# The instruction order of a two-block transformer kernel: a finer model in the ordering pass, and small matmuls issued in longer groups

## The chip, the core and the metric

The kernel runs on one core of one Trainium2 chip. The time is the device time of one execution in microseconds (us), the median of three runs. TensorE is PE in the profile (PEld are its weight loads), VectorE is DVE, ScalarE is ACT, GpSimd is POOL and SyncE, which issues the transfers here, is SP.

## The reference

Two transformer blocks work one after the other on x, 256 tokens of 1024 channels, in float32. The first block has two layers, the second one. Cut to what matters:

```python
for l in range(2):                       # first block
    z = rms_norm(x, norm1_g[l]) @ w_in[l]
    (cq, ckv, kpe, gq, gk, gv, glr, gr, su, gates) = split_in(z)
    o_a = mla_mixer(cq, ckv, kpe, ...)   # 8 heads of softmax attention
    o_b = gla_mixer(gq, gk, gv, glr, gr, ...)   # gated linear attention, 4 heads
    o_c = s5_mixer(su, ...)              # diagonal state space model + GLU
    g = sigmoid(gates + gate_b[l]).reshape(B, L, 3, D)
    x = x + (g0*(o_a @ w_br_mla) + g1*(o_b @ w_br_gla) + g2*(o_c @ w_br_s5)) @ w_out[l]
    x = x + square(relu(rms_norm(x, norm2_g[l]) @ w_ff1[l])) @ w_ff2[l]
# second block
q, k, v, glu_in, z_ga, z_gc = split(rms_norm(x, g_pre_mix) @ w_in_2)
y_attn = dilated_attention_mixer(q, k, v, rel_bias_table, w_attn_out)   # 24 heads in 3 groups
y_conv = conformer_conv_mixer(glu_in, ...)  # GLU, 31-tap causal conv, layer norm, silu, matmul
x = x + rms_norm((sigmoid(z_ga)*y_attn + sigmoid(z_gc)*y_conv) @ w_mix_out, g_post_mix)
x = x + rms_norm(swiglu_ffn(rms_norm(x, g_pre_ffn), ...), g_post_ffn)
```

## The kernel before

All big weights come as one stream of units, at most 128x1024 float32 each, in the order in which they are used. SP loads a unit into a tile `raw` (three buffers), ACT rounds it to the type fp32r as `wH` (L160, or L163 where a gain is multiplied in), and DVE makes the rest `wL = raw - wH` (L161, L164); `wH` and `wL` have four buffers each. Each product then takes three fp32r matmuls: high by high, high by low, low by high. L169 to L171 (`mm_f`) write 256 columns, L175 to L177 (`mm_t`) 512, and L1551 to L1553 are those of the convolution's output. Up to three units are fetched ahead (`AHEAD`).

Everything else on PE is plain float32 and small: transposes against the identity, attention scores and values, GLA's chunks, the S5 scan. This text calls those the small matmuls, and an unbroken row of them between two fp32r matmuls a run. They use PSUM tiles of one bank each from three pools: `mm` (2, the fp32r column units), `acc` (5) and `tr` (1).

What sets the order: `plan_layer` and `plan_second` walk the hand-written token lists `SCHED` and `SCHED2`. A token is a weight unit (`g1_6`, `co4`) or one step of a chain, and a chain is a generator that yields between steps: `l` GLA, `a` and `b` the two halves of the first block's attention, `s` S5, `h` the second block's attention, `c` the convolution, `n` its layer norm. The order in which instructions are written gives their priorities; the framework's ordering pass then plays the program through with a model of the engines and gives each engine, whenever it is free there, the ready instruction of best priority. So the order on an engine is not that of the text, and what a model believes to be ready decides it. On the chip each engine runs its list strictly in that order.

The small matmuls that the change touches, by function:

- `s5_tile_prep` (L466): eight transposes of `s5ep` (L478) in two groups of four, each into the one `tr` tile; ACT copies a group out to `ET` (L480) before the next can be written. Then eight small matmuls against `s5F` (L490).
- `gla` (L645), end: four transposes of `gla_og` per token half (L759).
- `mla_attn` (L861): per pair of heads four transposes of the q rows, copied out by ACT (L875), then four of the k rows (L872), through the one `tr` tile; scores (L884, L885); softmax; three transposes of `mla_p` per head (L906), copied out by L908; values (L912).
- `attn2` (L1401): per pair of heads and each of three groups, three transposes of the probabilities `sp` per head (L1448), copied out by L1450, then the values (L1457). L1436 is the exponential there, L1440 the scaling.

`mla_kv_evac` (L844) makes the normed k rows `mla_kn`: squares on ACT, the sum on DVE (L849), the inverse root on POOL (`rsq`, L184), two products on DVE (L856, L857). `s5_gelu` (L613) makes `s5gH` and `s5gL` for the S5 gate units (L621 to L627). `conv_gen` runs the 31 taps on DVE (L1321, L1318, L1314) with some products on ACT; `conv_ln` (L1352) norms the result: column sums (L1346), squares (L1363), the variance (L1349), the inverse root on POOL, its broadcast through PE (`tok_bcast`, L1333), a product on DVE (L1375), silu on ACT (L1378), and then the split `cH`, `cL` that the output units (L1551) read.

`k.behind(first, second)` adds a dependence: `second` becomes ready only after `first`.

Of the kernel before, what the change touches and what calls it, by code (L numbers as in the profile page):

```python
# [458 lines left out]
def s5_expand(k, dst, src):  # L459

    for g in range(2):
        rows, cols = slice(64 * g, 64 * g + 64), slice(16 * g, 16 * g + 16)
        k.nc.scalar.activation(dst[rows, :, :, cols], src[rows], AF.Copy)


def s5_tile_prep(k, st, ct):  # L466

    nc = k.nc
    js = slice(8 * ct, 8 * ct + 8)
    ep = k.s5ep  # L470
    s5_expand(k, ep[:, :, 0:1], st.b[:, js].unsqueeze(2))
    s5_expand(k, ep[:, :, 1:4], s5_powers(k, st, "s5e", 3, st.b, st.bs, ct, OP.add))
# [12 lines left out]
    s5_expand(k, k.s5F[:, :, 1:5], st.F[ct])  # L485
    Fq = k.s5F.rearrange("p (q c) s i -> p q c (s i)", c=2)
    ps = k.tr_tile()
    for c in range(2):
        for q in range(4):
            nc.tensor.matmul(ps[32 * q:32 * q + 32, 0:128], epq[:, q, c, 0:32], Fq[:, q, c, 0:128],  # L490
                             start=(c == 0), stop=(c == 1))
# [153 lines left out]
def gla(k, l, st):  # L645
# [97 lines left out]
    for tt in range(2):  # L743
# [8 lines left out]
        for h in range(4):  # L752
            hs = slice(h * P, (h + 1) * P)
            nc.vector.scalar_tensor_tensor(og[:, hs], po(tt, h), rs[:, h:h + 1], st.sr[:, tt, hs],
                                           op0=OP.mult, op1=OP.mult)
        yield
        pt = k.tr_tile()
        for h in range(4):
            nc.tensor.transpose(pt[:, h * P:(h + 1) * P], og[:, h * P:(h + 1) * P], k.ident)  # L759
# [83 lines left out]
def mla_kv_evac(k, l, st, t, ps, v):  # L843
# [13 lines left out]
    nc.vector.tensor_tensor(kn[:, :, 64:96], bcm(st.kr[:, t], 4), bcl(rh, 32), op=OP.mult)  # L857
# [4 lines left out]
def mla_attn(k, l, st, hf):  # L862

    nc = k.nc
    scale = 96.0 ** -0.5
    for pr in range(2):
        qk = []
        for src, g in ((st.qn[hf], "qhg"), (st.kn[hf], "khg")):
            ps = k.tr_tile()
            for hh in range(2):  # L870
                for t in range(2):
                    nc.tensor.transpose(ps[0:96, (2 * hh + t) * P:(2 * hh + t + 1) * P],  # L872
                                        src[t][:, 2 * pr + hh, :], k.ident)
# [5 lines left out]
        qT, kT = qk  # L879
        po = k.acc_tile()  # L880
        pb = []
        for hh in range(2):
            ps = k.acc_tile()
            nc.tensor.matmul(ps[:, 0:P], qT[0:96, hh, 0:P], kT[0:96, hh, 0:P], start=True, stop=True)  # L884
            nc.tensor.matmul(ps[:, P:3 * P], qT[0:96, hh, P:S], kT[0:96, hh, :], start=True, stop=True)  # L885
            sn = k.t2("mla_sn")
            mn = k.sm(2, "mmn")
            nc.vector.tensor_tensor_reduce(sn[:, 0:P], ps[:, 0:P], k.cmask[:, P:S], -scale, BIG, OP.add, OP.min,
                                           mn[:, 0:1])
            nc.vector.tensor_tensor_reduce(sn[:, P:3 * P], ps[:, P:3 * P], k.cmask, -scale, BIG, OP.add, OP.min,  # L890
                                           mn[:, 1:2])
            p = k.t2("mla_p")
            sm = k.sm(2, "msm")
            for b, cs in enumerate((slice(0, P), slice(P, 3 * P))):
                nc.scalar.activation(p[:, cs], sn[:, cs], AF.Exp, scale=-1.0, bias=mn[:, b:b + 1],
                                     accum_out=sm[:, b:b + 1])
            nc.vector.reciprocal(sm, sm)
            for b, cs in enumerate((slice(0, P), slice(P, 3 * P))):
                nc.vector.tensor_scalar(p[:, cs], p[:, cs], sm[:, b:b + 1], None, op0=OP.mult)
            pb.append(p)  # L900
            yield
        pTs = []
        for hh in range(2):
            pt = k.tr_tile()
# [4 lines left out]
        yield  # L909
        for j, (o, cs) in enumerate((((slice(0, S)), slice(0, S)), (slice(P, S), slice(S, 3 * P)))):  # L910
            for hh in range(2):
                k.behind(last, nc.tensor.matmul(po[64 * hh:64 * hh + 64, o], st.v[:, j, 4 * hf + 2 * pr + hh, :],  # L912
                                                pTs[hh][:, cs], start=(j == 0), stop=(j == 1)))
        yield
        k.split(st.moH[:, 2 * hf + pr], st.moL[:, 2 * hf + pr], po[:, 0:S])
        yield
# [485 lines left out]
def attn2(k, st, sp):  # L1402
# [28 lines left out]
    for i in hs:  # L1431
# [7 lines left out]
        for b, cs in enumerate(blocks):  # L1439
            nc.scalar.activation(s[i][:, :, cs], s[i][:, :, cs], AF.Copy, scale=sm[:, b:b + 1])  # L1440
        yield
    po = k.acc_tile()
    for g in range(3):
        pT = []
        for i in hs:
            pt = k.tr_tile()
            for b in range(3):
                nc.tensor.transpose(pt[:, b * P:(b + 1) * P], s[i][:, g, b * P:(b + 1) * P], k.ident)  # L1448
            pT.append(k.t2("pT2"))
            last = nc.scalar.activation(pT[i][:, 0:384].rearrange("p (b c) -> p b c", b=3)[:, :, ::-1],  # L1450
                                        pt[:, 0:384].rearrange("p (b c) -> p b c", b=3), AF.Copy)
        yield
        v = st.v2[g]
        for j, (o, cs) in enumerate(((slice(0, S), slice(0, S)), (slice(P, S), slice(S, 3 * P)))):
            for i in hs:
                h = 2 * sp + i
                k.behind(last, nc.tensor.matmul(po[rows[i], o], v[:, j, 64 * h:64 * h + 64], pT[i][:, cs],  # L1457
                                                start=(g == 0 and j == 0), stop=(g == 2 and j == 1)))
        yield
# [542 lines left out]
```

## Time and profile before

| | |
|---|---|
| median of 3 runs | 1453.17 us (1452.96 to 1453.40) |
| the profiled execution | 1451.78 us, of it span 1450.0 us |
| PE busy | 1402.2 us (97%), 10412 matmuls |
| DVE busy | 1012.9 us (70%) |
| ACT busy | 835.1 us (58%) |
| DMA | 243.1 MB, mean 168 GB/s |

A busy PE in this profile is an upper bound: matmuls overlap, so the length of one is more than the distance to the next. What a run of small matmuls costs is therefore read from the starts of the fp32r matmuls around it.

### The profile page before, as it was taken

The page shows a single profiled execution, that of the slowest core. Times are in us where ns is not written, and L with a number is a line of the kernel's source. Part 1 is how long each engine was busy: PE and PEld are TensorE (multiplying, and loading weights), DVE is VectorE, ACT ScalarE, POOL GpSimd, SP SyncE. Part 2 cuts the span into 40 slices and gives each one's busy share as a digit, 9 for nine tenths or more (in the row PEclk, how much of TensorE's full clock was granted, in tenths as well). Part 3 has the DMA queues.
Part 4 walks back from the last instruction along what each step waited for, and adds up shares of the span by engine and source line. Part 5 has one row for each costly group of instructions (what it writes and reads, how often), then busy time and mean ns, then how long its engine had stood idle before and what let it go on. Part 6 is the DMA issues. An engine that isn't in the chain of part 4 may idle for free.

```text
span 1450.0 us, 26147 instructions
## 1 busy us (share of the span) xinstructions
PE 1402.2 (97%) x10412; PEld 1272.1 (88%) x10412; DVE 1012.9 (70%) x1860; ACT 835.1 (58%) x1455; POOL 46.3 (3%) x51
## 2 busy tenths in 40 slices
PE   8999999999999999989999999999999999899998
PEld 6989889888899899888988999989888989689997
DVE  6987776689455667766566555579999846655555
ACT  6865566467754555455546444465678574544443
POOL 1000100000000000111000000000000000000000
PEclk9999999999999999999999999999999999999999
DMA  6622344555445552344456555565555445365553
GB/s 221 218 88 90 119 169 151 175 189 177 159 172 185 201 175 77 116 147 160 148 188 225 186 185 189 189 227 183 181 152 171 150 153 183 117 218 189 185 183 112
DMA packets 71058, 243.10 MB, mean 168 GB/s; under 512 B 7864, under 2 KB 11656, under 8 KB 70936
## 3 DMA queue, kind: packets, MB, share of 16 engines
q1 hardware_dynamic: 70936, 241.43, 48.8%
q8 instruction: 81, 1.33, 0.4%
q14 instruction: 41, 0.34, 0.1%
HBM read 237.17 MB, written 4.23 MB: 166 GB/s over the span
## 4 chain that ended last, share of the span: by engine, by line
PE 62%; DVE 13%; ACT 7%; issue 3%; DMA 2%; POOL 2%; POOLq 0%; DVEq 0%; ACTq 0%; SPq 0%
PE mm L169 11%; PE mm L171 11%; PE mm L170 11%; PE acc L175 7%; PE acc L177 7%; PE acc L176 7%; DVE wL L161 4%; ACT wH L160 2%; DVE cv L1321 2%; POOL rsq L184 2%; DMA raw<-in_wst_dram 2%; ACT sp L1436 1%; PE acc L553 1%; PE acc L1457 1%; ACT sp L1440 1%
## 5 line engine op out<-in xcount | busy, mean ns | idle before, releaser
L161 DVE TENSOR_TENSOR wL<-raw,wH 128x1024 fp32r<-128x1024 f32 (+1 forms) x410 | 496.1, 1211 | 260.4 <-ACT wH L160 259.0
L160 ACT ACTIVATE wH<-raw 128x1024 fp32r<-128x1024 f32 (+1 forms) x410 | 429.1, 1048 | 379.5 <-PE mm L170 184.7
L169 PE MATMUL mm<-hH,wH 128*128 128x256 f32 x1792 | 515.5, 288 | 5.0 <-ACT gt L1065 3.5
L171 PE MATMUL mm<-hH,wL 128*128 128x256 f32 x1792 | 510.4, 285 | 0.0
L170 PE MATMUL mm<-hL,wH 128*128 128x256 f32 x1792 | 509.7, 284 | 0.0
L169 PEld LDWEIGHTS mm<-hH,wH 128*128 128x128 f32 x1792 | 342.8, 191 | 17.2 <-issue 4.4
L170 PEld LDWEIGHTS mm<-hL,wH 128*128 128x128 f32 x1792 | 343.2, 191 | 3.6 <-issue 0.4
L171 PEld LDWEIGHTS mm<-hH,wL 128*128 128x128 f32 x1792 | 342.9, 191 | 1.4 <-issue 0.9
L175 PE MATMUL acc<-wH,fH 128*128 128x512 f32 x344 | 135.2, 393 | 0.0
L176 PE MATMUL acc<-wL,fH 128*128 128x512 f32 x344 | 134.8, 392 | 0.0
L177 PE MATMUL acc<-wH,fL 128*128 128x512 f32 x344 | 134.2, 390 | 0.6 <-DVE fL L161 0.6
L1321 DVE SCALAR_TENSOR_TENSOR cv<-u,ppt,cv 128x256 f32<-128x256 f32 x184 | 78.0, 478 | 0.3
L177 PEld LDWEIGHTS acc<-wH,fL 128*128 128x128 f32 x344 | 64.6, 188 | 15.2 <-DVE fL L161 1.1
L175 PEld LDWEIGHTS acc<-wH,fH 128*128 128x128 f32 x344 | 64.9, 189 | 11.4 <-ACT fH L160 0.2
L176 PEld LDWEIGHTS acc<-wL,fH 128*128 128x128 f32 x344 | 64.9, 189 | 10.5
L160 ACT ACTIVATE fH<-ffr 128x256 fp32r<-128x256 f32 x56 | 23.4, 417 | 68.4 <-DVE ffr L1224 68.4
L161 DVE TENSOR_TENSOR fL<-ffr,fH 128x256 fp32r<-128x256 f32 x56 | 23.7, 424 | 23.0 <-ACT fH L160 23.0
L176 PE MATMUL acc<-wL,hH 128*128 128x512 f32 x96 | 37.9, 398 | 0.9 <-DVE wL L161 0.9
L175 PE MATMUL acc<-wH,mH 128*128 128x512 f32 x96 | 37.8, 394 | 0.0
L176 PE MATMUL acc<-wL,mH 128*128 128x512 f32 x96 | 37.8, 394 | 0.0
L175 PE MATMUL acc<-wH,hH 128*128 128x512 f32 x96 | 37.8, 399 | 0.0
L177 PE MATMUL acc<-wH,hL 128*128 128x512 f32 x96 | 37.7, 396 | 0.0
(435 smaller groups left out, 2171.3 us busy)
## 6 DMA issues: line engine op xcount, KB each, us to landing
raw<-in_wst_dram SPq DMA_DIRECT2D x420, 512.0 KB, 3.5
xd<-x SPq DMA_DIRECT2D x6, 512.0 KB, 4.0
x<-xd SPq DMA_DIRECT2D x6, 512.0 KB, 5.7
bias<-bdram SPq DMA_DIRECT2D x8, 384.0 KB, 6.2
gnorm<-in_rows_dram SPq DMA_DIRECT2D x3, 512.0 KB, 5.3
raw<-in_wst_dram SPq DMA_DIRECT2D x4, 384.0 KB, 3.5
x<-in_x_dram SPq DMA_DIRECT2D x4, 256.0 KB, 4.5
x<-in_x_dram SPq DMA_DIRECT2D x2, 512.0 KB, 5.2
```

Of the source, the lines that this page charges most:

```text
L160: nc.scalar.activation(H, src, AF.Copy)
L161: nc.vector.tensor_sub(L, src, H)
L169: nc.tensor.matmul(ps, H[:, w], aH[:, i, :], start=(i == 0), stop=False)
L170: nc.tensor.matmul(ps, H[:, w], aL[:, i, :], start=False, stop=False)
L171: nc.tensor.matmul(ps, L[:, w], aH[:, i, :], start=False, stop=(i == nk - 1))
L175: nc.tensor.matmul(ps, aH[:, ki, tt], H[:, cols], start=start, stop=False)
L176: nc.tensor.matmul(ps, aH[:, ki, tt], L[:, cols], start=False, stop=False)
L177: nc.tensor.matmul(ps, aL[:, ki, tt], H[:, cols], start=False, stop=stop)
L184: nc.gpsimd.tensor_tensor(o, m, k.mhalf[:, 0:1].to_broadcast([P, n]), op=OP.pow)
L553: nc.tensor.matmul(ps[:, (4 * c + q) * 64:(4 * c + q + 1) * 64], E[:, c, :], us[:, q, :], start=True, stop=True)
L1321: nc.vector.scalar_tensor_tensor(st.cv[:, ct], u(ct, i), w(ct, i), st.cv[:, ct], op0=OP.mult, op1=OP.add)
L1436: nc.scalar.activation(s[i][:, :, cs], s[i][:, :, cs], AF.Exp, scale=-1.0, bias=mj[:, b:b + 1], accum_out=sm[:, b:b + 1])
```

## The change

It does three things. The context is opened with `schedule_with_timeline_sim=True`: the ordering pass then plays the program through with its finer timing model. Second, small matmuls that were written in two groups through one PSUM tile are written in one group through two, one `tr` and one `acc` tile, before either is copied out. Third, each matmul of a group waits, by `behind`, for the last value that any of the group needs (`made`, `scaled`, `last`), so that the pass cannot place the first ones earlier by themselves; in the first block's attention the q rows' transposes so wait for `mla_kn`. The attentions' steps are also written in another order (the next transposes ahead of the present values). The arithmetic, the weight stream, the token lists and the numbers of instructions stay as they are.

```diff
+    made = s5_expand(k, ep[:, :, 1:4], s5_powers(k, st, "s5e", 3, st.b, st.bs, ct, OP.add))
     epq = ep.rearrange("p (q c) s i -> p q c (s i)", c=2)
+    pts = [k.tr_tile(), k.acc_tile()]
     for hq in range(2):
-        ps = k.tr_tile()
         for qq in range(2):
             for c in range(2):
-                nc.tensor.transpose(ps[:, (2 * qq + c) * P:(2 * qq + c + 1) * P], epq[:, 2 * hq + qq, c], k.ident)
+                k.behind(made, nc.tensor.transpose(pts[hq][:, (2 * qq + c) * P:(2 * qq + c + 1) * P],
+                                                   epq[:, 2 * hq + qq, c], k.ident))
+    for hq in range(2):
+        ps = pts[hq]
         E = k.main.tile([P, 2, 2, P], F32, tag="gt", name="ET")
         nc.scalar.activation(E.rearrange("p a b c -> p (a b c)"), ps, AF.Copy)
         st.ET[2 * ct + hq] = E
     yield
...
+            made = nc.vector.scalar_tensor_tensor(og[:, hs], po(tt, h), rs[:, h:h + 1], st.sr[:, tt, hs],
+                                                  op0=OP.mult, op1=OP.mult)
...
+            k.behind(made, nc.tensor.transpose(pt[:, h * P:(h + 1) * P], og[:, h * P:(h + 1) * P], k.ident))
...
+    st.made = nc.vector.tensor_tensor(kn[:, :, 64:96], bcm(st.kr[:, t], 4), bcl(rh, 32), op=OP.mult)
...
+    made = st.made
...
+    def turn_qk(pr):
+        pts = [k.tr_tile(), k.acc_tile()]
+        for ps, src in zip(pts, (st.qn[hf], st.kn[hf])):
...
+                    k.behind(made, nc.tensor.transpose(ps[0:96, (2 * hh + t) * P:(2 * hh + t + 1) * P],
+                                                       src[t][:, 2 * pr + hh, :], k.ident))
+        qk[pr] = []
+        for ps, g in zip(pts, ("qhg", "khg")):
             dst = k.t2("mla_T", (P, 2, S))
             nc.scalar.activation(dst[0:96].rearrange("p a b -> p (a b)"), ps[0:96], AF.Copy,
                                  scale=k.pp(g, l)[0:96, :])
-            qk.append(dst)
...
+    def turn_p(pr):
+        pts = [k.tr_tile(), k.acc_tile()]
+        for hh in hs:
             for b in range(3):
-                nc.tensor.transpose(pt[:, b * P:(b + 1) * P], pb[hh][:, b * P:(b + 1) * P], k.ident)
-            pTs.append(k.t2("mla_pT"))
-            last = nc.scalar.activation(pTs[hh][:, 0:384], pt[:, 0:384], AF.Copy)
-        yield
+                k.behind(last[pr], nc.tensor.transpose(pts[hh][:, b * P:(b + 1) * P],
+                                                       pbs[pr][hh][:, b * P:(b + 1) * P], k.ident))
+        pTs[pr] = []
+        for hh in hs:
+            pTs[pr].append(k.t2("mla_pT"))
+            last[pr] = nc.scalar.activation(pTs[pr][hh][:, 0:384], pts[hh][:, 0:384], AF.Copy)
...
+    turn_qk(0)
+    yield
+    pss = scores(0)
+    turn_qk(1)
+    softmax(0, pss[0])
+    yield
+    softmax(0, pss[1])
+    yield
+    turn_p(0)
+    yield
+    values(0)
+    pss = scores(1)
+    softmax(1, pss[0])
+    yield
+    evac(0)
+    softmax(1, pss[1])
+    yield
...
+            scaled = nc.scalar.activation(s[i][:, :, cs], s[i][:, :, cs], AF.Copy, scale=sm[:, b:b + 1])
...
+    def turn(g):
+        pTs[g] = []
+        pts = [k.tr_tile(), k.acc_tile()]
...
+                k.behind(scaled, nc.tensor.transpose(pts[i][:, b * P:(b + 1) * P], s[i][:, g, b * P:(b + 1) * P],
+                                                     k.ident))
+        for i in hs:
+            pTs[g].append(k.t2("pT2"))
+            last[g] = nc.scalar.activation(pTs[g][i][:, 0:384].rearrange("p (b c) -> p b c", b=3)[:, :, ::-1],
+                                           pts[i][:, 0:384].rearrange("p (b c) -> p b c", b=3), AF.Copy)
...
+    turn(0)
+    yield
+    yield
+    po = k.acc_tile()
+    turn(1)
+    values(0)
+    yield
+    yield
+    turn(2)
+    values(1)
+    yield
+    values(2)
+    yield
...
-    with _tile.TileContext(nc) as tc:
+    with _tile.TileContext(nc, schedule_with_timeline_sim=True) as tc:
```

The built order shows 205 runs of small matmuls on PE before and 135 now: 160 and 102 ahead of the first tap of the convolution, 38 and 27 from there to its output units, 7 and 6 after. Three places follow. Line numbers of the changed kernel are higher: L880 is L872, L893 and L894 are the scores L884 and L885, L853 to L861 are L849 to L857, L625, L626 and L629 are L621, L622 and L625, L1393 is L1349, L1377 is L1333, L1466 and L1468 are the second attention's scores L1422 and L1424, L1613 is L1551.

PE, layer 0 of the first block, where the first half's attention starts (`mla_qn`, `mla_kn`: normed q and k rows). Before:

```order
L170 MATMUL mm<-hL,wH 128x256
L171 MATMUL mm<-hH,wL 128x256
L872 MATMUL tr<-cst,mla_qn 96x128 x4
L169 MATMUL mm<-hH,wH 128x256
L170 MATMUL mm<-hL,wH 128x256
```

Now:

```order
L171 MATMUL mm<-hH,wL 128x256
L880 MATMUL tr<-cst,mla_qn 96x128 x4
L880 MATMUL acc<-cst,mla_kn 96x128 x4
L880 MATMUL tr<-cst,mla_qn 96x128 x4
L893 MATMUL acc<-mla_T 128x128
L894 MATMUL acc<-mla_T 128x256
L893 MATMUL acc<-mla_T 128x128
L894 MATMUL acc<-mla_T 128x256
L880 MATMUL acc<-cst,mla_kn 96x128 x4
L169 MATMUL mm<-s5gH,wH 128x256 x2
```

The q rows' transposes stood alone between fp32r matmuls; now they stand with the k rows' and the scores in one run of twenty, and the next fp32r matmuls are those of the S5 gate, which read `s5gH` and `s5gL`.

DVE at the same place. Before:

```order
L621 TENSOR_SCALAR s5w<-s5w 128x1024
L851 TENSOR_SCALAR kss<-kss 128x4
L622 TENSOR_TENSOR s5w<-s5w,s5y 128x1024
L854 TENSOR_SCALAR krc<-rsq_2222,mla_rs 128x4
L857 TENSOR_TENSOR mla_kn<-kr,rsq_2222 128x4x32
L856 TENSOR_TENSOR mla_kn<-acc,krc 128x4x64
L161 TENSOR_TENSOR wL<-raw,wH 128x1024
L625 SCALAR_TENSOR_TENSOR s5g_2235<-s5w,s5y 128x1024
L161 TENSOR_TENSOR wL<-raw,wH 128x768
L164 SCALAR_TENSOR_TENSOR s5gL<-s5g_2235,s5gH 128x1024
```

Now:

```order
L161 TENSOR_TENSOR wL<-raw,wH 128x1024
L853 TENSOR_REDUCE kss<-mla_sq 128x4
L854 TENSOR_SCALAR kss<-kss,mla_rs_1477,ssk 128x4
L625 TENSOR_SCALAR s5w<-s5w 128x1024
L855 TENSOR_SCALAR kss<-kss 128x4
L626 TENSOR_TENSOR s5w<-s5w,s5y 128x1024
L858 TENSOR_SCALAR krc<-rsq_2222,mla_rs 128x4
L861 TENSOR_TENSOR mla_kn<-kr,rsq_2222 128x4x32
L860 TENSOR_TENSOR mla_kn<-acc,krc 128x4x64
L629 SCALAR_TENSOR_TENSOR s5g_2235<-s5w,s5y 128x1024
L164 SCALAR_TENSOR_TENSOR s5gL<-s5g_2235,s5gH 128x1024
```

The two weight splits that stood between the k rows and `s5gL` now stand further up, so PE has their units behind it when it comes to the k rows; the split at the top waits for the last fp32r matmul ahead of PE's run.

PE, second block, the layer norm's broadcast (`diag`) and what follows it. Before:

```order
L171 MATMUL mm<-hH,wL 128x256
L1333 MATMUL acc<-diag,cst 128x128
L1422 MATMUL acc<-k,q 128x128 x2
L1333 MATMUL acc<-diag,cst 128x128
L1424 MATMUL acc<-k,q 128x256 x2
L169 MATMUL mm<-hH,wH 128x256
L170 MATMUL mm<-hL,wH 128x256
```

Now:

```order
L171 MATMUL mm<-hH,wL 128x256
L1393 MATMUL tr<-cst,cs_13369 128x1 x2
L1377 MATMUL acc<-diag,cst 128x128
L1466 MATMUL acc<-k,q 128x128 x2
L1468 MATMUL acc<-k,q 128x256 x2
L1377 MATMUL acc<-diag,cst 128x128
L1613 MATMUL mm<-cH,wH 128x256 x2
```

Before, four units of 24 fp32r matmuls and some small ones stood between the broadcast and the first output unit, and two units between the variance (L1349) and the broadcast; now the three follow each other directly, and those units stand ahead of them.

## Rows read from the trace of the kernel before

**Rows 1.** The page: busy time, share of the span and instructions of each engine
```profile
PE 1402.2 (97%) x10412; PEld 1272.1 (88%) x10412; DVE 1012.9 (70%) x1860; ACT 835.1 (58%) x1455; POOL 46.3 (3%) x51
```

**Rows 2.** Windows (length, busy PE, PEld, DVE, ACT, POOL, PE clock, DMA): the convolution
```profile
984.00:1140.00 156.00, 152.96 (x1182) 140.79 (x1181) 153.66 (x343) 105.63 (x192) 0.00 (x0) 1.00 0.52 171
```

**Rows 3.** Timeline of PE (start us, length us, what): one run of four transposes
```profile
237.52 0.28 PE L170 MATMUL mm<-hL,wH 128*128 128x256 f32 x1
237.81 0.64 PE L872 MATMUL tr<-cst,mla_kn 128*96 128x128 f32 x4
...
238.41 0.28 PE L169 MATMUL mm<-hH,wH 128*128 128x256 f32 x1
```

**Rows 4.** Timeline of PE: a run of value matmuls alone
```profile
254.72 0.28 PE L170 MATMUL mm<-hL,wH 128*128 128x256 f32 x1
254.98 0.87 PE L912 MATMUL acc<-mla_pT,mla_v 128*64 128x256 f32 x8
...
256.00 0.28 PE L169 MATMUL mm<-hH,wH 128*128 128x256 f32 x1
```

**Rows 5.** Timeline of PE: the two kinds in one run
```profile
189.94 0.28 PE L171 MATMUL mm<-hH,wL 128*128 128x256 f32 x1
190.21 0.87 PE L912 MATMUL acc<-mla_pT,mla_v 128*64 128x256 f32 x8
191.01 0.64 PE L872 MATMUL tr<-cst,mla_qn 128*96 128x128 f32 x4
...
191.61 0.28 PE L170 MATMUL mm<-s5gL,wH 128*128 128x256 f32 x1
```

**Rows 6.** Waits of PE: who, for whom, us in total, times, longest
```profile
PE mm L169 <- ACT gt L1065: 3.5, 2, 1.8
PE tr L478 <- ACT ET L480: 3.1, 4, 1.4
PE tr L906 <- DVE mla_p L899: 2.4, 2, 1.6
...
PE tr L759 <- DVE gla_og L754: 1.9, 2, 1.0
...
PE tr L478 <- ACT s5ep L463: 1.8, 2, 1.6
PE tr L872 <- ACT mla_T L875: 1.8, 2, 1.0
```

**Rows 7.** Timeline of DVE (in brackets idle time and its end): k rows, S5 gate
```profile
175.14 1.21 DVE L161 TENSOR_TENSOR wL<-raw,wH 128x1024 fp32r<-128x1024 f32 x1
...
180.24 0.42 DVE L856 TENSOR_TENSOR mla_kn<-acc,krc 128x256 f32<-128x256 f32 x1
...
184.05 1.23 DVE L164 SCALAR_TENSOR_TENSOR s5gL<-s5g,s5gH 128x1024 fp32r<-128x1024 f32 x1 [0.23 <-ACT s5gH L163]
```

**Rows 8.** Timeline of ACT: silu, exponentials and table loads ahead of `cH`
```profile
1162.24 1.28 ACT L1378 ACT_TABLE_LOAD   x1
1163.53 0.60 ACT L1378 ACTIVATE cv<-cv,ppt 128x256 f32<-128x256 f32 x1
...
1171.04 1.43 ACT L1440 ACTIVATE sp<-sp,asm 128x384 f32<-128x384 f32 x2
...
1177.73 1.08 ACT L1378 ACTIVATE cv<-cv,ppt 128x256 f32<-128x256 f32 x2
...
1179.09 1.05 ACT L160 ACTIVATE cH<-cv 128x1024 fp32r<-128x1024 f32 x1
```

**Rows 9.** Timeline of DVE: the variance, and the norm's product
```profile
1155.70 0.16 DVE L1367 TENSOR_SCALAR var<-tr 128x2 f32<-128x2 f32 x1 [0.25 <-PE tr L1349]
...
1162.05 1.22 DVE L1375 TENSOR_TENSOR cv<-cv,acc 128x1024 f32<-128x1024 f32 x1 [0.58 <-PE acc L1333]
```

**Rows 10.** Windows, as in rows 2: around the wait for `cH`
```profile
1160.00:1179.40 19.40, 16.67 (x134) 15.06 (x133) 9.36 (x20) 18.43 (x32) 0.00 (x0) 1.00 0.38 129
1179.40:1186.20 6.80, 6.64 (x31) 5.31 (x31) 2.13 (x2) 5.28 (x10) 0.00 (x0) 0.50 0.09 34
```

More of the change, by code (lines that the diff above doesn't have):

```diff
@@ L462, in s5_expand @@
         rows, cols = slice(64 * g, 64 * g + 64), slice(16 * g, 16 * g + 16)
-        k.nc.scalar.activation(dst[rows, :, :, cols], src[rows], AF.Copy)
+        last = k.nc.scalar.activation(dst[rows, :, :, cols], src[rows], AF.Copy)
+    return last
 def s5_tile_prep(k, st, ct):
@@ L489, in s5_tile_prep @@
         for q in range(4):
-            nc.tensor.matmul(ps[32 * q:32 * q + 32, 0:128], epq[:, q, c, 0:32], Fq[:, q, c, 0:128],
-                             start=(c == 0), stop=(c == 1))
+            k.behind(made, nc.tensor.matmul(ps[32 * q:32 * q + 32, 0:128], epq[:, q, c, 0:32],
+                                            Fq[:, q, c, 0:128], start=(c == 0), stop=(c == 1)))
     for q in range(4):
@@ L876, in mla_attn @@
                                  scale=k.pp(g, l)[0:96, :])
-            qk.append(dst)
-        yield
[L879 to L901, printed above, removed]
@@ L914, in mla_attn, with scores, softmax @@
-        yield
-        k.split(st.moH[:, 2 * hf + pr], st.moL[:, 2 * hf + pr], po[:, 0:S])
-        yield
+            qk[pr].append(dst)
+    def scores(pr):
+        qT, kT = qk.pop(pr)
+        pss = [k.acc_tile() for _ in hs]
+        for hh in hs:
+            nc.tensor.matmul(pss[hh][:, 0:P], qT[0:96, hh, 0:P], kT[0:96, hh, 0:P], start=True, stop=True)
+            nc.tensor.matmul(pss[hh][:, P:3 * P], qT[0:96, hh, P:S], kT[0:96, hh, :], start=True, stop=True)
+        return pss
+    def softmax(pr, ps):
+        sn = k.t2("mla_sn")
+        mn = k.sm(2, "mmn")
+        nc.vector.tensor_tensor_reduce(sn[:, 0:P], ps[:, 0:P], k.cmask[:, P:S], -scale, BIG, OP.add, OP.min,
+                                       mn[:, 0:1])
+        nc.vector.tensor_tensor_reduce(sn[:, P:3 * P], ps[:, P:3 * P], k.cmask, -scale, BIG, OP.add, OP.min,
+                                       mn[:, 1:2])
+        p = k.t2("mla_p")
+        sm = k.sm(2, "msm")
+        for b, cs in enumerate(blocks):
+            nc.scalar.activation(p[:, cs], sn[:, cs], AF.Exp, scale=-1.0, bias=mn[:, b:b + 1],
+                                 accum_out=sm[:, b:b + 1])
+        nc.vector.reciprocal(sm, sm)
+        for b, cs in enumerate(blocks):
+            last[pr] = nc.vector.tensor_scalar(p[:, cs], p[:, cs], sm[:, b:b + 1], None, op0=OP.mult)
+        pbs.setdefault(pr, []).append(p)
@@ L920, with evac @@
+    def evac(pr):
+        k.split(st.moH[:, 2 * hf + pr], st.moL[:, 2 * hf + pr], pos[pr][:, 0:S])
+    turn_qk(0)
[16 more added lines that the diff above has]
+    yield
+    turn_p(1)
+    yield
+    values(1)
+    yield
+    evac(1)
+    yield
 class TAcc:
@@ L1456, in attn2 @@
                 h = 2 * sp + i
-                k.behind(last, nc.tensor.matmul(po[rows[i], o], v[:, j, 64 * h:64 * h + 64], pT[i][:, cs],
-                                                start=(g == 0 and j == 0), stop=(g == 2 and j == 1)))
-        yield
+                k.behind(last[g], nc.tensor.matmul(po[rows[i], o], v[:, j, 64 * h:64 * h + 64], pTs[g][i][:, cs],
+                                                   start=(g == 0 and j == 0), stop=(g == 2 and j == 1)))
+    turn(0)
[4 more added lines that the diff above has]
+    values(0)
+    yield
+    yield
+    turn(2)
+    values(1)
+    yield
+    values(2)
+    yield
     k.split(st.aoH[:, sp], st.aoL[:, sp], po[:, 0:S])
```

44 lines of the change are left out of this document (14 added, 30 removed).

## The prediction

> **What bounds the kernel now.** First the page: PE is busy for 97% of the span, the next engine, DVE, for 70% [rows 1]. So nearly everywhere the time is what PE issues, and a change of order helps only by shorter switches on PE or fewer waits of PE. The exception is found with the windows: through the convolution's taps DVE is busy for 153.66 of 156 us and PE for 152.96 of the same 156 [rows 2], so there neither has room. A difference of 2.9 us, 0.2%, is about what a measurement of this kernel can tell from no change. The profiled execution took 1451.78 us, 1.4 less than the median of 1453.17; the terms below come from it, and their sum is put on the median.
>
> **1. Fewer runs: -15.** The price of a switch is read from the starts of the fp32r matmuls around a run. In the timeline two of 256 columns that follow each other start 0.12 us apart. Four transposes between two of them make it 0.89 (237.52 to 238.41 [rows 3]): one entry and one exit, each with the gap it replaces, so the run costs 0.65 over two pitches of 0.12. Eight value matmuls alone take 254.72 to 256.00 [rows 4], 1.28, or 1.04 over two pitches. Both kinds in one run take 189.94 to 191.61 [rows 5], 1.67, or 1.43. Apart they cost 0.65 + 1.04 = 1.69, together 1.43: a run that is merged saves 0.26. The lower bound is the entry alone: from the last fp32r matmul to the first of the run 0.27 us pass in place of 0.12 [rows 5], so 0.15. The order has 58 runs fewer ahead of the taps (160 to 102): 58 x 0.26 = 15.1 us, with 8.7 as the other end. I take 0.26, since it is measured on the kinds that the change gathers most. The 11 fewer in the convolution stretch are counted at 3 below, the one fewer behind it at nothing.
>
> **2. Waits inside the gathered groups: -11, and -3.5.** With two PSUM tiles the second group of S5's transposes no longer waits for the first copy (L478 on `ET`, 3.1 us in four waits), and the k rows no longer for the copy of the q rows (L872, 1.8). And with the `behind` edges the groups are ordered behind their data: L478 on `s5ep` 1.8, L906 on `mla_p` 2.4, L759 on `gla_og` 1.9. Together 11.0 us [rows 6], if other matmuls cover what was waited for; 4.9 of it, the two that lose their buffer wait, should go in any case, so the ends are -4.9 and -11. The two waits of L169 for `gt` (3.5 us [rows 6]) stand at the places of part 4 and vanish in what is put there.
>
> **3. Convolution and its norm: 0.** From the variance to the end of `cH` it takes 1155.70 to 1180.14 now, 24.4 us [rows 8, 9]. In the changed order broadcast and product follow the variance without units between. From the variance to the product's start it is 6.35 now [rows 9]; I take 4 where only the chain is left. Then the product, 1.22 [rows 9], and on ACT what stands ahead of `cH`: six silu of about 0.5 each (3.1), a table load of 1.28, two exponentials and two scalings (2.9, two pairs at the 1.43 of a pair of scalings), another load of 1.28, two silu 1.08, `cH` 1.05 [rows 8], 10.7 in all. 4 + 1.2 + 10.7 = 15.9, some 8.5 less than now. Against that four units more stand ahead of the variance. Their splits add 4 x 1.22 = 4.9 to a DVE that is full there [rows 2, 9], the splits being as long as that product; if PE is what counts, they add 4 x 24 x 0.12 = 11.5, less 11 merged runs x 0.26 = 2.9, so 8.6. The column sums and squares ahead of the variance I put 4 later, because splits are interleaved with them. DVE's sum is 4.9 + 4 - 8.5 = +0.4, PE's 8.6 + 4 - 8.5 = +4; with the sums unmoved DVE's is -3.6. I take 0, and keep -4 and +9 (the norm's gain half lost as well). PE will stand some 14 us there, far more than the 2.7 it lacks in 1160 to 1179.4 now [rows 10], but for work that it has behind it.
>
> The load and the first activation behind it begin 1.28 us apart, 1162.24 and 1163.53 [rows 8], and I take that. The Trainium skill (ScalarE: Activation LUTs, What ACT_TABLE_LOAD costs) adds a drain of about 1.38 us to each switch; by that the two loads inside this chain would make `cH` 2.8 us later and the predicted time 1447 in place of 1444.5. The trace disagrees: the gap between load and activation is 0.01 us.
>
> **4. New waits: +21.** At layer 0's k rows PE's units have moved ahead, as the order shows, and it must wait for `mla_kn`. On DVE the split that waits for PE's last matmul started at 175.14 now and the second product ended at 180.66 [rows 7], 5.5 us. Within the run of twenty the scores wait for copies on ACT, as L872 does now with up to 1.0 [rows 6], so I take 7. The ends are 1.8, the longest wait for `gt` now [rows 6], and 10.1, up to the end of `s5gL` at 185.28 [rows 7], which the S5 gate behind the run reads. Layer 1 has the same chain with the GLA rows beside it: 6, since it has no S5 gate right behind it. Then I count some 13 smaller places in the order where the fp32r matmul behind a longer run reads a value that was made just before (`s5us` twice, GLA's and the attention's rounded outputs, weight splits that come late): at 0.6 each, the size of the waits now (L872's two make 1.8, L759's two 1.9 [rows 6], some of it covered), 8. So 7 + 6 + 8 = 21, with ends of 5 and 31. SP's queue of loads keeps its order and its count; it runs up to three units ahead, so I cost its moved issues at nothing. If that cover went, the waits would show on `wH`.
>
> **Sum.** -15.1 - 11.0 - 3.5 + 0 + 21 = -8.6, on the median 1444.6.
>
> **The rivals.** (a) *The new waits don't come.* The finer model may know the chains' lengths so well that what looks bare in the order is ready in time. Then parts 1 and 2 stand almost alone: -29.6, with two or three us of waits left about 1427. For it: the model was made for this, and most of the PE waits in the list are under 2 us [rows 6]. Against it: at the k rows and at the norm the order has no fp32r matmul left to cover anything.
>
> (b) *Nothing comes of it.* The new waits eat the gain: at parts 1 and 2 at their lower ends (8.7 + 4.9 + 3.5 = 17) against 17 to 20 of new waits the time is 1453. For it: covered waits tend to turn up a little later on an engine that is 97% busy. Against it: the merged runs' gain does not depend on any wait.
>
> (c) *Slower: PE runs ahead and stands.* The splits are ordered ahead of the chains, so PE uses up its units and then stands at the k rows of both layers, at the norm and at the small places, and after a long stand it issues at the lower clock. For it: after the wait that ends with `cH` the granted clock is 0.50, 1.2 GHz instead of 2.4, for 6.80 us of almost full work (6.64 [rows 10]), which costs 3.4. With 10 + 7 at the k rows, 13 x 0.8 = 10 at the small places, 6 of 9 lost at the norm and two more such stretches at 3.4 it is 40 against 29.6 gained, +10, 1463. It decides once the stands and slow stretches sum to more than about 30 us. Against it: one such stretch exists now and is in the 1453 already.
>
> The Trainium skill (TensorE: Matmul & The Clock Gate, Why this matters for your kernels) warns of idle gaps between bursts of matmuls, after which the engine is at the lower clock; by that rule the two k-row stands would be followed by slow stretches too, which is (c). The trace agrees at the wait for `cH`, and shows no stand as long as the new ones elsewhere.
>
> **How the numbers follow.** Forecast, 1431 to 1450: 0.46. (a), below 1431: 0.14. (b), within 2.9 us of the median: 0.14. (c), above 1456: 0.26. So faster 0.60, same 0.14, slower 0.26. From 1425 to 1462 the range holds the forecast, (b), most of (a) and about half of (c); of both tails a little under 2 in 10 is left out. The likeliest case's own range is 1431 to 1450.
>
> **What would show it.** The list of PE's waits: L478 on `ET` and L906 on `mla_p` gone; new ones at the first L880 of a layer on `mla_kn` of 5 to 7 us, and at L1613 on `cH` of some 10 to 14. The timeline: single runs of four transposes replaced by runs of twelve and twenty, with entry and exit as now. The windows: in the convolution DVE full as before and its end about 5 us later, the clock 0.50 behind `cH` as now. I am wrong on the size of the gain if the merged runs leave the fp32r matmuls the same total distance; on the sign if clock below 1.00 shows behind the k rows of both layers, or if the convolution's end moves by more than 9 us.

## The result and the profile after

The changed kernel takes **1516.44 us** (median of 4 runs, 1512.32 to 1518.12) against 1453.29 of the kernel before in the same session: a ratio of 1.043, 95% interval 1.0405 to 1.045. It is 63 us slower; the prediction said 1444.6, and its range ended at 1462.

The page of the profile after, its span, the busy row of the engines and the granted clock in 40 slices:

```profile
span 1516.3 us, 26180 instructions
...
PE 1425.2 (94%) x10412; PEld 1292.2 (85%) x10412; DVE 1012.8 (67%) x1860; ACT 832.3 (55%) x1455; POOL 39.4 (3%) x51
...
PEclk9989999999999999899999999999999969899999
```

The span is 66.3 us longer than the 1450.0 of before. PE's busy time rose from 1402.2 [rows 1] to 1425.2, by 23.0; the rest of the span, in which PE does nothing, from 47.8 to 91.1, by 43.3. The matmuls are the same 10412, so the 23.0 is slower work: the mean granted clock fell from 0.991 to 0.970. At two levels, 1.0 and 0.5, that is 26 us at half clock before (2 x 0.009 x 1450) and 91 now (2 x 0.030 x 1516); half of the 65 more would be 32, and part of it PE stood. Inside the stretches at half clock PE was busy for 17.7 us before and 61.2 now; half of the 43.5 more is 21.7, so the clock accounts for nearly all of the 23.0.

PE's waits after, as in [rows 6]:

```profile
PE mm L1613 <- ACT cH L160: 13.8, 1, 13.8
PE tr L880 <- DVE mla_kn L861: 6.3, 1, 6.3
...
PE tr L549 <- ACT s5w L498: 3.8, 2, 3.0
PE acc L880 <- DVE mla_kn L861: 3.5, 1, 3.5
PE acc L1377 <- DVE diag L1376: 3.4, 2, 2.2
PE acc L557 <- ACT s5us L552: 3.4, 2, 2.5
PE acc L175 <- ACT hH L163: 3.3, 5, 1.2
PE tr L918 <- DVE mla_p L911: 2.9, 2, 1.9
```

The new waits that the prediction named are there, at the k rows and at `cH`. Beside them stand a dozen of 1 to 4 us that it counted at 0.6 each or not at all: at S5's tables (L549, L557) and where a normed input is handed to the next product (`hH`, `diag`). Summed by the value that was waited for, some 61 us of PE's waits are new or longer and 20 are gone. The wait of S5's transposes on `ET` is gone, that on `mla_p` is not.

Where the time went is read by taking the fp32r matmuls in order, since both kernels issue 8304 of them through the same weight stream, and comparing the start of the n-th:

| from to (n-th fp32r matmul) | part | later by then, us | in this part |
|---|---|---|---|
| 0 to 1512 | layer 0: attention, GLA, S5 | 19.6 | +19.6 |
| 1512 to 2592 | its feed-forward | 24.3 | +4.7 |
| 2592 to 4104 | layer 1: attention, GLA, S5 | 35.0 | +10.7 |
| 4104 to 5256 | its feed-forward, next norm | 41.9 | +6.9 |
| 5256 to 5400 | second block, first values | 48.0 | +6.1 |
| 5400 to 6624 | up to the norm's broadcast | 45.7 | -2.3 |
| 6624 to 6768 | the wait for `cH` | 63.3 | +17.6 |
| 6768 to the end | the rest | 63.9 | +0.6 |

Long stretches of weight units run at exactly the old pace: 94 us of the first feed-forward, 144 of the second and the last 145 before the end. The loss lies in the stretches where the chains' small matmuls stand among them. Windows of the kernel after (columns as in [rows 2]), the stretches with the most time at half clock, with the one ahead of the third, and the taps:

```profile
83.50:93.80 10.30, 8.54 (x37) 8.36 (x38) 6.38 (x11) 4.57 (x8) 0.00 (x0) 0.50 0.14 51
199.60:206.40 6.80, 5.76 (x22) 4.65 (x23) 3.75 (x10) 4.11 (x6) 0.53 (x1) 0.50 0.00 0
...
1223.60:1247.50 23.90, 9.35 (x39) 7.88 (x40) 6.86 (x19) 16.78 (x27) 0.00 (x0) 0.50 0.19 66
1012.50:1202.00 189.50, 185.44 (x1409) 170.19 (x1407) 172.62 (x371) 119.81 (x215) 0.00 (x0) 0.99 0.52 170
...
612.40:619.40 7.00, 7.00 (x62) 6.95 (x60) 4.59 (x11) 1.68 (x5) 0.00 (x0) 1.00 0.48 152
619.40:629.70 10.30, 10.30 (x112) 8.89 (x112) 3.79 (x13) 0.87 (x5) 1.12 (x1) 0.50 0.01 2
```

The half-clock stretches shown lie at the stands (S5's tables at 83.5, the k rows of layer 0 at 199.6, `cH` at 1223.6), but for one: at 619.4 PE had been busy for all of the 7 us before, and was for all of it. Of the eight others, of 3.4 to 10.2 us, seven have a wait of PE of over 1 us in or just ahead of them, and the last is the end, where PE has no more work. The taps take 189.5 us from first to last now. The same stretch of the kernel before took 170.0:

```profile
969.00:1139.00 170.00, 166.96 (x1298) 154.79 (x1297) 165.44 (x364) 115.42 (x208) 0.00 (x0) 1.00 0.54 178
```

What holds up the taps is seen in DVE's groups over that stretch (line, engine, operation, tiles, shapes, count, busy us, mean ns of one, idle time before them and what ended it), first before:

```profile
L1321 DVE SCALAR_TENSOR_TENSOR cv<-u,ppt,cv 128x256 f32<-128x256 f32 x184 | 78.0, 478 | 0.3
L161 DVE TENSOR_TENSOR wL<-raw,wH 128x1024 fp32r<-128x1024 f32 x50 | 60.8, 1219 | 2.9 <-ACT wH L160 2.8
```

and after:

```profile
L1365 DVE SCALAR_TENSOR_TENSOR cv<-u,ppt,cv 128x256 f32<-128x256 f32 x184 | 79.6, 481 | 0.4
L161 DVE TENSOR_TENSOR wL<-raw,wH 128x1024 fp32r<-128x1024 f32 x54 | 66.1, 1223 | 12.5 <-ACT wH L160 12.0
```

Four splits more stand among the taps, 5.3 us, and DVE stands 12.0 us instead of 2.8 in front of splits whose rounding on ACT isn't there yet, with the taps queued behind.

### The profile page after: what moved, and what is told of

Read it like the earlier page. It is cut to its first block, busy times and chain, and to the rows that moved or that the text cites. A ratio compares the mean times of both kernels' runs of the same rounds, so it can differ in the third digit from the quotient of the medians.

```text
span 1516.3 us, 26180 instructions
## 1 busy us (share of the span) xinstructions
PE 1425.2 (94%) x10412; PEld 1292.2 (85%) x10412; DVE 1012.8 (67%) x1860; ACT 832.3 (55%) x1455; POOL 39.4 (3%) x51
## 5 line engine op out<-in xcount | busy, mean ns | idle before, releaser
L175 PE MATMUL acc<-wH,fH 128*128 128x512 f32 x344 | 131.2, 394 | 0.6 <-ACT fH L160 0.4
L177 PE MATMUL acc<-wH,fL 128*128 128x512 f32 x344 | 129.7, 392 | 0.0
L176 PEld LDWEIGHTS acc<-wL,fH 128*128 128x128 f32 x344 | 65.4, 190 | 12.3 <-DVE wL L161 1.6
L164 DVE SCALAR_TENSOR_TENSOR wL<-raw,ppt,wH 128x512 fp32r<-128x512 f32 x40 | 28.4, 748 | 13.1 <-ACT wH L163 13.0
L163 ACT ACTIVATE wH<-raw,ppt 128x512 fp32r<-128x512 f32 x40 | 26.5, 716 | 18.2 <-PE acc L177 9.1
```

Source lines behind the costliest of these rows:

```text
L163: nc.scalar.activation(H, src, AF.Copy, scale=scale)
L164: nc.vector.scalar_tensor_tensor(L, src, scale, H.bitcast(F32), op0=OP.mult, op1=OP.subtract)
L175: nc.tensor.matmul(ps, aH[:, ki, tt], H[:, cols], start=start, stop=False)
L176: nc.tensor.matmul(ps, aH[:, ki, tt], L[:, cols], start=False, stop=False)
L177: nc.tensor.matmul(ps, aL[:, ki, tt], H[:, cols], start=False, stop=stop)
```

## The experiments

| kernel | median, us | ratio to before (95%) | clock | span less PE busy |
|---|---|---|---|---|
| before | 1450.6 to 1453.6 | 1 | 0.991 | 47.8 |
| changed | 1516.44 | 1.0428 (1.0405 to 1.0450) | 0.970 | 91.1 |
| e1, finer model alone | 1519.26 | 1.0460 (1.0429 to 1.0491) | 0.968 | 98.2 |
| e2, gathering alone | 1448.14 | 0.9971 (0.9959 to 0.9983) | 0.994 | 48.2 |
| e3, e2 without the new dependences | 1449.67 | 0.9977 (0.9965 to 0.9989) | 0.989 | 47.4 |
| e4, changed without them | 1511.55 | 1.0406 (1.0389 to 1.0423) | 0.973 | 89.4 |
| e5, changed, PE near the written order | 1566.62 | 1.0785 (1.0760 to 1.0811) | 0.958 | 127.2 |
| e6, changed, units held back at the norm | 1512.94 | 1.0418 (1.0387 to 1.0448) | 0.974 | 85.0 |
| e7, as e5 in the first block alone | 1556.62 | 1.0713 (1.0671 to 1.0755) | 0.949 | 117.5 |
| e8, e1, PE near the written order | 1597.98 | 1.1009 (1.0982 to 1.1037) | 0.947 | 155.5 |
| e9, e1 with the old order of DVE | 1577.18 | 1.0854 (1.0828 to 1.0881) | 0.960 | 129.2 |
| e10, e1 with the old order of PE | 1535.75 | 1.0567 (1.0547 to 1.0588) | 0.970 | 103.7 |
| e11, e1 with the old order of ACT | 1568.81 | 1.0805 (1.0783 to 1.0826) | 0.967 | 127.4 |
| e12, old order of all three | 1457.25 | 1.0029 (1.0014 to 1.0045) | 0.989 | 50.2 |
| e13, old order of DVE and ACT | 1568.87 | 1.0819 (1.0776 to 1.0863) | 0.963 | 125.1 |
| e14, old order of PE and DVE | 1498.04 | 1.0328 (1.0313 to 1.0344) | 0.979 | 79.7 |
| e15, old order of PE and ACT | 1519.81 | 1.0481 (1.0459 to 1.0502) | 0.978 | 91.0 |

The time of before is the range of its medians over the five sessions; each ratio is to the kernel before in the same session. Clock and the last column are of the profiled execution.

### The two halves of the change: e1 to e4

e1 is the kernel before with one line changed, e2 the changed kernel with that line undone:

```diff
-    with _tile.TileContext(nc) as tc:
+    with _tile.TileContext(nc, schedule_with_timeline_sim=True) as tc:
```

> The kernel before with nothing changed but the ordering pass's finer model. Theory A (the finer model's order is what costs: it moves fp32r units ahead of the chains, PE stands, and issues at the half clock behind each stand): 1500 to 1515 us, mean granted clock about 0.97, one wait for cH of over 10 us at the convolution's output units. Theory B (the gathering costs: a group that waits for its last value leaves PE bare): 1445 to 1456 us, clock 0.99, no wait for cH over 2 us. Theory C (only both together cost): also near 1453.

> The changed kernel with the ordering pass's old model, so the gathering, its dependences and the new order of the attentions' steps alone. The built order has 148 runs of small matmuls, against 205 before and 135 in the changed kernel. Theory A: 57 runs fewer at up to 0.26 us and the waits inside the groups gone, 1430 to 1445 us, clock 0.99. Theory B: 1500 us or more, clock 0.97. Theory C: 1430 to 1450.

e3 and e4 take the new dependences out of the six places (the two older ones at the values stay; `free` hands back its second argument and adds nothing):

```diff
-                k.behind(made, nc.tensor.transpose(pts[hq][:, ...
+                free(made, nc.tensor.transpose(pts[hq][:, ...
```

> As the gathering alone, but the new dependences between a group's matmuls and the last value that any of them needs are taken out; each still waits for its own data. 174 runs of small matmuls. If the dependences are what makes PE stand, this is faster than the gathering with them; if they only save switches, it is slower by about 26 runs x 0.26 = 7 us or less.

> The changed kernel, finer model kept, without those new dependences (153 runs). Theory A: still 1500 to 1515 us, with the wait for cH of over 10 us. Theory B or C with the dependences as the cause: 1450 to 1465.

Theory A holds for the time, with e1 4 us above its range: the finer model alone costs 4.6%, the gathering alone gains 0.3%, and together they cost about what the model costs. Its sign, the long wait for `cH`, is there in e1:

```profile
PE mm L1551 <- ACT cH L160: 13.4, 1, 13.4
```

In e4 it did not come as expected: there that wait is 3.6 us, PE waits 8.8 us in one piece for an attention's `sp` instead, and the time is still 1512. So this one wait is not the loss; where the order makes PE stand differs from kernel to kernel. The dependences do nothing that can be measured (the intervals of e2 and e3 overlap, and so do those of e4 and the changed kernel). e2 is 4 us faster than the kernel before, a small gain, but its interval is clear of 1; 8 to 23 were expected. Its waits of PE at the k rows:

```profile
PE tr L880 <- DVE mla_kn L861: 4.5, 2, 2.6
...
PE acc L880 <- DVE mla_kn L861: 2.2, 1, 2.2
```

6.7 us, in a kernel whose PE is idle no less than before (48.2 and 47.8): some 15 us of its waits went, and 15 of others came.

Next to nothing is saved on the switches either. Four transposes of `s5ep` in the timeline of the kernel before (start us, length us), in a place where PE waits for nothing:

```profile
68.21 0.28 PE L170 MATMUL mm<-hL,wH 128*128 128x256 f32 x1
68.39 0.66 PE L478 MATMUL tr<-cst,s5ep 128*128 128x128 f32 x4
68.80 0.36 PE L171 MATMUL mm<-hH,wL 128*128 128x256 f32 x1
```

and eight in one run in e2:

```profile
347.75 0.40 PE L177 MATMUL acc<-wH,fL 128*128 128x512 f32 x1
347.99 0.60 PE L479 MATMUL tr<-cst,s5ep 128*128 128x128 f32 x4
348.43 0.60 PE L479 MATMUL acc<-cst,s5ep 128*128 128x128 f32 x4
348.78 0.37 PE L169 MATMUL mm<-hH,wH 128*128 128x256 f32 x1
348.98 0.28 PE L170 MATMUL mm<-hL,wH 128*128 128x256 f32 x1
```

Start to start it is 0.59 and 1.03. Less the one pitch that is there anyway (0.12 and 0.227 us), four cost 0.47 here and eight 0.80. The first fp32r matmul behind a run also holds up the next: here 348.78 to 348.98, 0.20 in place of 0.12, so the full price is read at the second one behind. Over all runs of these two kinds at full clock in which PE stands nowhere for more than 0.15 us, it is 0.45 for four (median of 6, before) and 0.88 for eight (median of 4, e2): two groups of four cost 0.89, one of eight 0.88. Such a run costs its transposes, 0.11 us each, and next to nothing for the switch.

### Holding PE back: e5 to e8

Counted in the built orders, a small matmul has on average 20.6 fp32r matmuls ahead of it that were written behind it in the kernel before, and 53.7 in the changed kernel. So the next theory was that PE spends its weight units ahead of the chains and has none left when it must wait. e5, e7 and e8 hold it near the written order (`ORDER_ONLY` stands here for a dependence of order without a wait on a semaphore; `LAG` is 1; `LO` and `HI` bound the units that are held, in e7 those of the first block):

```diff
+        if lhs.dtype == F32R:
+            if k.fresh:                      # a unit's first matmul
+                k.fresh = False
+                k.marks.append(k.last_small)
+                if LO <= len(k.marks) < HI and not 139 <= len(k.marks) < 146 and len(k.marks) > LAG and k.marks[-1 - LAG] is not None:
+                    tc.add_manual_dep(r.ins, k.marks[-1 - LAG].ins.name, ORDER_ONLY)
```

> The changed kernel with the finer model, but PE's order is held near the written one: the first fp32r matmul of a weight unit may not be ordered ahead of a small matmul that was written before the unit ahead of it (seven units at the change from layer 0 to layer 1 left free). In the built order a small matmul then has 14.6 fp32r matmuls ahead of it on average that were written behind it, against 53.7 in the changed kernel and 20.6 before; DVE and ACT keep the finer model's order of their own. Theory D (the whole loss is that PE's units run ahead of the chains): 1445 to 1465 us, clock 0.985 or more. Theory E (it is the order on DVE and ACT, which put the chains' steps late): 1490 to 1520 us.

> As e5_lag1, in the first block alone (its 276 weight units). The curves of the changed kernel and the one before part by about 38 us in the first block and by 26 in the second. Theory D: 1478 to 1490 us. Theory E: 1510 or more.

> The kernel before with the finer model and PE held near the written order as in e5_lag1, without the gathering (15.0 fp32r matmuls ahead on average). Theory D: 1448 to 1465 us against 1519 of the finer model alone, and within 8 us of e5_lag1, as the gathering is worth little. Theory E: 1490 to 1520.

> The changed kernel with one edit: the four units written between the layer norm's variance and its broadcast may not be ordered ahead of the variance's matmuls; in the built order they then stand between the variance and the first output unit, 96 fp32r matmuls of 0.12 us, 11.5 us. Theory D: the wait for cH falls from 13.8 to 2 to 5 us, the half-clock stretch around it (23.9 us long) goes or is cut to 7, so the time falls by 10 to 16 us, to 1500 to 1506. Theory E: the wait for cH stays and the same work is late in another place: 1512 to 1518.

```diff
+            if i == 0 and k.gate is not None:      # zc5, zc7, zc4, zc0: behind the variance's matmul
+                order_after(k.gate, r)
```

All of theory D fell: 1567, 1557 and 1598 us, slower than without the hold. Theory E's 1490 to 1520 was missed by e5 and e8 too, so the hold itself costs; DVE and ACT were ordered anew around the held PE, and these runs do not show what PE's place alone is worth. e6 is the clearest, and its time lies in theory E's range. The wait for `cH` is gone, as theory D expected, but the time fell by 3.5 us (with overlapping intervals), not by 10 to 16. Its waits show one in its place:

```profile
PE tr L1502 <- ACT sp L1493: 5.4, 3, 4.9
```

and on DVE the chain ends hardly sooner. Variance and `cL` in the changed kernel, then in e6:

```profile
1221.70 0.16 DVE L1411 TENSOR_SCALAR var<-tr 128x2 f32<-128x2 f32 x1 [0.40 <-PE tr L1393]
...
1240.78 1.23 DVE L161 TENSOR_TENSOR cL<-cv,cH 128x1024 fp32r<-128x1024 f32 x1 [3.18 <-ACT cH L160]
```

```profile
1213.59 0.16 DVE L1420 TENSOR_SCALAR var<-tr 128x2 f32<-128x2 f32 x1 [1.17 <-PE tr L1401]
...
1236.02 1.22 DVE L161 TENSOR_TENSOR cL<-cv,cH 128x1024 fp32r<-128x1024 f32 x1
```

e6 is 3.3 us ahead all along in this execution, from before the place. Put on one clock the variance is 4.8 us earlier and `cL` 1.5: with units between them it takes 22.4 us from one to the other instead of 19.1. From there to the end e6 is 7.1 us ahead in this execution, 3.8 more than before the place. So the stand of 13.8 us at `cH` is the place where a chain of DVE and ACT that is late already ends; filling it with units that PE would do anyway gains 4 us and does not move the chain.

### One engine in the old order: e9 to e15

The program texts of e1 and of the kernel before are the same, so their instructions have the same numbers. These kernels are e1 with a table of the numbers in which an engine's instructions stand in the kernel before, and a dependence of order from each to the next:

```diff
+def _impose(nc, tc):
+    traced = {i.name: i for i in nc.cur_bb.bb.instructions}
+    dep = mybir.DependencyInfo(mybir.DependencyClass.NoSync, mybir.DependencyReason.DATA)
+    for order in ORDERS:
+        names = [f"I-{n}" for n in order if f"I-{n}" in traced]
...
+        for a, b in zip(names, names[1:]):
+            tc.add_manual_dep(traced[b], a, dep)
```

e9 has DVE's table, e10 PE's, e11 ACT's, e12 all three, e13 to e15 the pairs. In the traces PE and ACT have the old order throughout wherever their table is in, and DVE has it for all but at most 4 of 1860 instructions; in e12 the order on PE, DVE, ACT and POOL is that of the kernel before, instruction by instruction.

> The kernel before with the finer model (1519 us), but DVE's instructions are chained in the order that they have in the kernel before (a table of their numbers; 1780 of 1860); the other engines keep what the finer model then gives them. Theory F (weight splits stand at the head of DVE's queue, wait for ACT's rounding, and hold up the chains behind them): 1455 to 1480 us, the taps of the convolution back to 170 us. Theory G (PE's order alone, which has 44 fp32r matmuls ahead of a small one here against 21 before, is the cost): 1500 us or more. Theory H (the loss lies in how the engines' orders fit together, so one restored order does not help): 1490 to 1520, and only all of them give 1453.

> As e9_order_dve, but PE's matmuls alone are chained in the order of the kernel before (20.6 fp32r matmuls ahead of a small one, as before); DVE and ACT keep the finer model's choice. Theory F: 1490 us or more. Theory G: 1450 to 1470. Theory H: 1490 to 1520 or more, as holding PE near the written order gave 1567.

> As e9_order_dve, but ACT's instructions alone are in the order of the kernel before. If the late weight roundings on ACT are what DVE waits for, 1455 to 1485 us. Theory F with the splits' place on DVE as the cause, and theory G: 1500 or more.

> DVE, ACT and PE all in the order of the kernel before, under the finer model. All theories: 1450 to 1458 us, which shows that the chains of numbers cost nothing and that the order on these three is the whole of the loss; if it stays above 1460, the queues of SP and POOL, or the waits that the finer model lays between engines, hold a part.

> Finer model; DVE and ACT in the order of the kernel before, PE left to the model (35.5 fp32r matmuls ahead of a small one on average). Theory H1 (the loss is that the finer model sees PE at another pace than it has, so PE's own order is the wrong one and the others follow it): 1490 us or more, as PE still runs ahead. Theory H2 (the weight pipe, rounding on ACT and split on DVE, must keep its old order, and PE's does little): 1455 to 1470.

> Finer model; PE and DVE in the order of the kernel before, ACT left to the model. Theory H1: 1460 to 1490, as ACT then has only the copies and roundings to place. Theory H2: 1490 or more, as ACT's roundings come at other places than DVE's splits.

> Finer model; PE and ACT in the order of the kernel before, DVE left to the model. Theory H1: 1460 to 1490. Theory H2: 1490 or more.

All three together give 1457 us, inside the 1450 to 1458 that all theories expected: the order on PE, DVE and ACT is all but 4 us of the loss. The page of e12 is that of the kernel before again:

```profile
PE 1404.8 (97%) x10412; PEld 1275.0 (88%) x10412; DVE 1013.0 (70%) x1860; ACT 836.2 (57%) x1455; POOL 46.3 (3%) x51
```

Each alone makes it worse than 1519: PE 1536, ACT 1569, DVE 1577. So F and G both fell, and H is what is shown, though its range for e9 ended at 1520. Of the pairs only PE with DVE gains (1498, to which ACT adds the last 41); DVE with ACT, without PE, is as bad as each of them alone, and PE with ACT equals e1. Theory H1 expected 1460 to 1490 of both pairs with PE, and H2 1455 to 1470 of the pair without: neither holds. One sign of the mismatch is seen in ACT's group of roundings in e9, where DVE has the old order and ACT and SP do not (idle time before it last):

```profile
L160 ACT ACTIVATE wH<-raw 128x1024 fp32r<-128x1024 f32 (+1 forms) x410 | 429.5, 1049 | 478.2 <-issue 150.3 <-DMA raw<-in_wst_dram 133.9 <-PE mm L170 124.3
```

Before, the transfers are not among the first three causes of that group's idle time (379.5 us in all); here ACT stands 133.9 us for them. How much of the 1577 us that is, this does not show.

**What stays open.** Why the finer model chooses this order, that is, which of its durations differ from the chip's and by how much, was not tried. The experiments show that the order costs the time and that the three engines' orders only work together, not which estimate is behind it. With one engine's order fixed the model orders the others anew, so e9 to e15 are not a sum of parts.

## Why the prediction was wrong

**What bounds the kernel** was read rightly: PE, and in the taps DVE as well. That second part was the one to take further.

**Part 1, -15.1: the step that failed is the price of a merged run.** "A run that is merged saves 0.26" was taken from one row of each kind. Its measure is sound: up to the second fp32r matmul behind the run, less two pitches (the first one starts at 238.20 in [rows 3], 255.78 in [rows 4] and 191.41 in [rows 5]). By it, over all runs of the kernel before at full clock in which PE stands nowhere for more than 0.15 us, eight value matmuls cost 1.00 (median of 3; 1.04 in [rows 4]) and four transposes of the k rows 0.49 (median of 6, from 0.44 to 0.65; [rows 3] is the slowest). Both kinds in one run cost 1.38 (median of 5; 1.43 in [rows 5]). So this merger saves 0.11, and eight transposes in one run instead of two save 0.01. e2 has 57 runs fewer and gained 4 us in all; PE's busy time fell by 4.9 (1402.2 to 1397.3), 0.09 for each.

**Part 2, -11 and -3.5.** This part held by itself: 15 us of waits went in e2 and 20 in the changed kernel, S5's on `ET` (3.1) among them. In e2 some 15 of new ones came as well, 6.7 of them at the k rows, so PE's idle time did not change; part 4 had counted 21. With the gathering alone, then, it is part 1 that left the gain at 4 us.

**Part 3, 0: the step that failed is the cost of what stands ahead of the variance.** It was put at 4.9 on DVE, four splits, and 4 for the sums. Measured, the taps took 19.5 us longer: 7.2 of DVE's busy time (165.44 to 172.62), 5.3 of it the four splits, and 12.3 of idle time, of which the splits' waits for `wH` rose by 9.2. "PE will stand some 14 us there, but for work that it has behind it" was right for the length (13.8) and wrong for the cost: over the two parts of the table that hold the taps and the stand 15 us were lost (-2.3 and +17.6), so the work done ahead had not made up for it. From the variance to the end of `cH` it took 19.0 us rather than 15.9. DVE's product for the norm, and on ACT a table load and silu, then `cH`:

```profile
1227.58 2.34 DVE L1419 TENSOR_TENSOR cv<-cv,acc 128x1024 f32<-128x1024 f32 x2
```

```profile
1228.79 1.28 ACT L1422 ACT_TABLE_LOAD   x1
1230.08 3.05 ACT L1422 ACTIVATE cv<-cv,ppt 128x256 f32<-128x256 f32 x6
...
1239.70 1.04 ACT L160 ACTIVATE cH<-cv 128x1024 fp32r<-128x1024 f32 x1
```

To the product it took 5.9 instead of 4. A third table load, which the sum left out, stands between the product's first half and the first silu (1.3 us more). From the first silu to the end of `cH` it is 10.7, as forecast. The load at 1228.79 took 1.28 and the silu behind it began at 1230.08, 0.01 later, as before. So the drain that the Trainium skill adds (ScalarE: Activation LUTs, What ACT_TABLE_LOAD costs) does not show here either.

**Part 4, +21: the step that failed is the price of the small places.** The k rows came near the forecast, 6.3 and 3.5 us against 7 and 6. The 13 smaller places were put at 0.6 each, 8 in all. Of the 61 us of waits that are new or longer, 13.6 are for `cH` and 9.8 for the k rows; the other 37 are these places and hand-offs that nobody looked at in the order: S5's tables, the norms between attention and feed-forward, the start of the second block.

**What the sum had no term for** is the clock. PE's busy time rose by 23.0 with the same matmuls, nearly all of it at half clock; the prediction had 6.8 of this in rival (c) and nothing in its sum. With the 43.3 of idle time that makes the 66.3 by which the profiled span grew.

**The rivals.** (c) names the direction and the mechanism: PE stands, then issues at half clock. Its size was off: it counted 33 of lost stands and 6.8 at half clock, against 61 of new waits and 23. Two of its readings were off as well. It counts one slow stretch in the kernel before; the trace has five, 26.8 us in all (117.9, 626.4, 1179.4, 1251.1 and 1445.6). And the one at 1179.4 [rows 10] does not follow a wait for `cH`: PE waits 0.2 us for it there, and the longest stand just ahead, 1.7 us, is for `pT` (L1448). Both of its signs that the time would rise came true: the taps grew by more than 9 us, and the clock is 0.50 at the k rows of both layers, from 199.6 to 206.4 and from 663.8 to 670.6. These two agree with the sentence of the Trainium skill beside (c) (TensorE: Matmul & The Clock Gate, Why this matters for your kernels), on idle gaps between bursts of matmuls. (a) needed the new waits not to come, (b) needed some 20 us of them. That the finer model by itself orders worse, at many places beside the three that were looked at, was not among the rivals; e1 shows that it does, by 4.6%.

## What to carry to other kernels

When a change replaces what orders the whole program, three places of the order don't price it: count over every hand-off, on each engine, what stands between the producer and the reader, DVE's and ACT's queues as much as PE's. Take the price of a small effect from the median over all undisturbed instances, never from a single pair of rows. And the orders of the engines are fitted to one another: here the old order put back on one engine alone made the time worse each time, and on all three it gave the time back. So try the switch of the model by itself before anything is built on it.

## What the runs showed of the hardware

The clock also fell where PE did not stand: in the changed kernel it is 1.00 from 612.4 to 619.4 and 0.50 from 619.4 to 629.7, with PE busy for all of both. Of the 59 matmuls that start in the first stretch 42 are small ones, of the 110 in the second 96. The kernel before has the same once, from 117.9 to 121.3 us, with 88 small ones among the 111 of the 7 us ahead, 64 of them S5's. So a stand isn't the only thing that comes before half clock; what else does was not tried.

At full clock a transpose of 128x128 between fp32r matmuls costs 0.11 us in groups of four and of eight alike (0.45 and 0.88 us in all), so going from fp32r matmuls to plain float32 transposes and back has hardly a price of its own.
